# One-layer hybrid decoder with a mixture of experts on one core: gathers one block ahead in the first pair, a register load moved behind pair 10, squares summed on VectorE

## The chip, the cores and the metric

The kernel runs on one core of one Trainium2 chip. The metric is the device time of one execution in microseconds (us), the median of several runs. The engines are named as in the profile: PE is TensorE's matmul, PEld its weight load, DVE is VectorE, ACT is ScalarE, POOL is GpSimd, SP is SyncE, whose queue issues the loads of the weights here. A name with a q behind it (PEq, SPq) is an engine's sequencer: branches, register loads, issues of transfers.

## The reference

One layer is computed on 256 tokens of 1024 numbers:

```python
mod = silu(c) @ W_ada + b_ada            # shift, scale and gate of both sub-layers
h   = rmsnorm(x) * (1 + scale1) + shift1
proj = h @ w_in                          # 9224 columns: attention, mLSTM, gates
merged = sigmoid(g_a) * (y_a @ w_a) + sigmoid(g_b) * (y_b @ w_b)
x  += gate1 * (merged @ w_out)
h   = rmsnorm(x) * (1 + scale2) + shift2
x  += gate2 * moe(h)                     # the best 4 of 32 experts, clamped SwiGLU, D_FF = 1024
out = rmsnorm(x)                         # final norm
```

All of it is float32. What the change touches is the second norm (the mean of the squares of x over its 1024 channels), and the mixture of experts behind it.

## The kernel before

**Layout.** The residual stream lies transposed in `xT`, as KT = 8 blocks of 128 channels (on the partitions) by T = 256 tokens. A block is called kt.

**The w_out stage.** `merged @ w_out` is made in four chunks c of two blocks each. For each block the loop adds the gated product to `xT` (L754, DVE), scales it for the norm (L756, DVE), squares it into `sq` (L758, ACT), and then gives PE three things: the router's logits (L761, two matmuls that add up in one bank over the eight blocks), the mean of the squares (L765, two matmuls of `sq` with a column of 1/1024, also added up over the eight blocks), and the transposes of the scaled block (L768). The norm, the choice of the best four experts and the rank of each token in its expert follow on DVE, POOL, ACT and PE.

**The experts.** They are taken in 16 pairs. An expert has 64 slots in a pair's main pass; `G` (L819) is a matrix of ones and zeros that says which token sits in which slot. A pair p has these steps on PE:

- `biases`: four matmuls `s<-b1s,sel` that start the four banks of the first product with the bias;
- a gather per block (`pm<-G,mghi`), by which the slots' tokens are picked out of the normed rows `xn` (a tile called mghi), and which ACT copies to `XG[p]` with the shift added (L878);
- `first_product`: for each block and each half hf, four matmuls `s<-w,xg` with 128x512 of weights;
- SwiGLU on DVE and ACT, transposes, then `second_product`, 32 matmuls `t<-w,whi`;
- the scatter of the result to `xT` (`add_out`, matmuls `pm<-S,whi` and additions on DVE, L867), which is done during the first product of the next pair.

From pair 1 on, the gather of a pair is done in the pair ahead of it. In pair 0 there is no pair ahead: for each block the loop issues one gather and then the first product of this block. `pe()` keeps the matmuls of this part in the order in which the program gives them; all are recorded under L850.

**The weights.** A pair needs 12 loads of 2 MB: 8 for the first product (L949), 4 for the second (L954). They go by SP's queue, in order, into a ring of wide slots; a load waits on SP until the matmuls that read its slot before are done. Pair 0 is loaded apart, in halves (L943), since some of the ring's slots come free only during it. SP's instructions run in order, so a load that waits holds up all behind it.

**Further rounds.** An expert with over 64 tokens needs more slots. The largest count becomes `nit`, a number of rounds (L1066, DVE); `values_load` (L1067) reads it into a register on each of the five engines. Behind pair 10 (`REST_AT`) stands the branch that uses it (L1114): with zero rounds, as with these inputs, its body is skipped. Where nothing orders an instruction otherwise, a scheduler places it, for each engine apart.

Of the kernel before, what the change touches and what calls it, by code (L numbers as in the profile page):

```python
# [2 lines left out]

# [1 line left out]

# [5 lines left out]
F32 = mybir.dt.float32  # L14
# [5 lines left out]
OP = mybir.AluOpType  # L20
# [3 lines left out]
T = 256  # L24
D = 1024
KT = 8
# [37 lines left out]
def body(tc, a, out):  # L64
    nc = tc.nc
    mm = nc.tensor.matmul
    act = nc.scalar.activation
    tt = nc.vector.tensor_tensor
    ts = nc.vector.tensor_scalar
    stt = nc.vector.scalar_tensor_tensor  # L70
# [16 lines left out]
    def shaped(x, shape):  # L87

        n = int(np.prod(shape[1:]))
        names = "abc"[:len(shape) - 1]  # L90
        x = x[:, 0:n]
        if len(names) == 1:
            return x
        return x.rearrange(f"p ({' '.join(names)}) -> p {' '.join(names)}", **dict(zip(names[1:], shape[2:])))

    def next_wide():

        spare_half.clear()
        p = slots.pop(0)
        slots.append(p)  # L100
        return p.tile([128, 4 * D], F32, name="w")

    def next_slot(shape):

        if not spare_half:
            w = next_wide()
            spare_half.append(w[:, 2 * D:])
            return shaped(w, shape)
        return shaped(spare_half.pop(), shape)
# [8 lines left out]
    xT = const.tile([128, KT, T], F32, name="xT")  # L118
# [9 lines left out]
    mean = const.tile([128, 128], F32, name="mean")  # L128
# [10 lines left out]
    SH1, SC1, G1, SH2, SC2, G2 = range(6)  # L139
# [34 lines left out]
    for n in range(2):  # L174
        pz = ps_z.tile([128, 2, 512], F32, name="pz")[:, 0]
        b = slice(512 * n, 512 * n + 512)
# [22 lines left out]
    def mod_of(m, kt):  # L199
        return modT[:, 8 * m + kt:8 * m + kt + 1]  # L200
# [58 lines left out]
    def take():  # L259
        if not ready:  # L260
            fetch()
        return ready.pop(0)
# [255 lines left out]
    for c in range(4):  # L518
# [21 lines left out]
        for n in range(2):  # L540
# [22 lines left out]
            for x in (hi, lo):  # L563
                last = x is lo
# [78 lines left out]
    def read_out(hd, S):  # L643
        num = ps_z.tile([128, 2, 512], F32, name="pz")
        hn = mx.tile([128, 2, 256], F32, name="cs")
        st = mx.tile([128, 5, 2], F32, name="st")
        for t in range(2):
            for s in range(t + 1):
                mm(num[:, t, 0:257], S[:, 128 * t + 128 * s:128 * t + 128 * s + 128], ve[:, s, 0:257],
                   start=s == 0, stop=s == t)  # L650
        den = num[:, :, 256]
        stt(st[:, 0], den, -1.0, em[:, :, hd], OP.mult, OP.max)
        tt(st[:, 0], st[:, 0], den, OP.max)
        nc.vector.reciprocal(st[:, 1], st[:, 0])
        for t in range(2):
            sq = mx.tile([128, T], F32, name="sq")
            act(sq, num[:, t, 0:256], AF.Square, scale=st[:, 1, t:t + 1], accum_out=st[:, 2, t:t + 1])
        ts(st[:, 3], st[:, 2], 1.0 / 256, EPS, op0=OP.mult, op1=OP.add)
        nc.gpsimd.tensor_tensor(st[:, 3], st[:, 3], half, OP.pow)
        tt(st[:, 4], st[:, 1], st[:, 3], OP.mult)  # L660
        for t in range(2):
            ts(hn[:, t, :], num[:, t, 0:256], st[:, 4, t:t + 1], None, op0=OP.mult)
        return hn
# [15 lines left out]
    last = None  # L679
    for hd in range(4):  # L680
# [6 lines left out]
        last = hd, read_out(hd, S), so  # L687
# [41 lines left out]
    wk, c_wk = pool("wk", reuse_waits="tile")  # L729
# [3 lines left out]
    pl = ps_m.tile([128, 512], F32, name="pm")  # L733
# [9 lines left out]
    for c in range(4):  # L743
        w = take()
        if c < 3:
            ps = proj_T(w, (mghi, mglo))
            fetch()
            po = [ps[:, 0, :], ps[:, 1, :]]
        else:
            po = proj_apart(w, (mghi, mglo))  # L750
        px = ps1.tile([128, 512], F32, name=f"s{c}").rearrange("p (t n) -> p t n", t=2)
        for n in range(2):
            kt = 2 * c + n
            stt(xT[:, kt, :], po[n], mod_of(G1, kt), xT[:, kt, :], OP.mult, OP.add)  # L754
            x = xa[c // 2][:, kt % 4, :]
            ts(x, xT[:, kt, :], A2[:, kt:kt + 1], None, op0=OP.mult)  # L756
            sq = wk.tile([128, T], F32, name="GS"[n])
            act(sq, xT[:, kt, :], AF.Square)  # L758
            for t in range(2):
                b = slice(128 * t, 128 * t + 128)  # L760
                mm(pl[:, 32 * t:32 * t + 32], x[:, b], rw[:, kt, :], start=False, stop=kt == KT - 1,  # L761
                   skip_group_check=True)
            for t in range(2):
                b = slice(128 * t, 128 * t + 128)
                mm(pl[:, 96 + t:97 + t], sq[:, b], mean[:, 0:1], start=False, stop=kt == KT - 1,  # L765
                   skip_group_check=True)
            for t in range(2):
                nc.tensor.transpose(px[:, t, 128 * n:128 * n + 128], x[:, 128 * t:128 * t + 128], ident)  # L768
        if c < 3:
            act(xtok[c // 2][:, c % 2], px, AF.Copy)  # L770
        later((0,0,0,0,)[c])
# [53 lines left out]
    XG, SS, ROWS = {}, {}, {}  # L825
    G0, last = slots_of(0)
# [21 lines left out]
    def pe(*args, **kw):  # L848

        return tc.keep_in_program_order(mm(*args, **kw))  # L850
# [8 lines left out]
    def add_out(lhsT_of, rhs, groups=range(4)):  # L859

        for g in groups:
            p = ps_m.tile([128, 2, T], F32, name="pm")
            for j in range(2):
                pe(p[:, j, :], lhsT_of(2 * g + j), rhs, start=True, stop=True)
            for j in range(2):
                kt = 2 * g + j
                stt(xT[:, kt, :], p[:, j, :], mod_of(G2, kt), xT[:, kt, :], OP.mult, OP.add)  # L867

    def gather(kts, G, xg):

        width = G.shape[-1]
        p = ps_m.tile([128, 512], F32, name="pm")
        for j, kt in enumerate(kts):
            c = slice(128 * kt, 128 * kt + 128)
            for t in range(2):
                pe(p[:, width * j:width * j + width], xn[:, t, c], G[:, t], start=t == 0, stop=t == 1)
        for j, kt in enumerate(kts):
            act(xg[kt] if isinstance(xg, list) else xg[:, kt, :], p[:, width * j:width * j + width], AF.Identity, bias=mod_of(SH2, kt))  # L878
# [132 lines left out]
    def pair(p):  # L1011
        a1 = biases(p)
        aT = halves([128, 4, 128]) if p else None
        if p == 0:
            for kt in range(KT):
                gather((kt,), G0, XG[0])
                for hf in range(2):
                    first_product(p, a1, hf, kt)
            scatter_map(p)
            aT = halves([128, 4, 128])  # L1020
            ms = [hidden(a1, hf) for hf in range(2)]
            G, _ = slots_of(p + 1)
            gather(range(4), G, XG[p + 1])
            turn(ms[0], 0, aT)
            gather(range(4, 8), G, XG[p + 1])
            m = ms[1]
        else:
            for kt in range(KT):
                first_product(p, a1, 0, kt)
                if p - 1 in ROWS and 1 <= kt <= 4:  # L1030
                    scatter(p - 1, (kt - 1,))
            m = hidden(a1, 0)
            for kt in range(KT):
                first_product(p, a1, 1, kt)
                if kt == 1:
                    scatter_map(p)
                if kt == 3:
                    turn(m, 0, aT)
            m = hidden(a1, 1)
            G, _ = slots_of(p + 1)  # L1040
            for q in range(2):
                gather(range(4 * q, 4 * q + 4), G, XG[p + 1])
        a2 = [ps2.tile([128, 512], F32, name=f"t{n}") for n in range(2)]
        for kt in range(KT):
            if kt == 4:
                turn(m, 1, aT)
            second_product(p, a2, aT, kt)
        ROWS[p] = out_rows(a2)
# [12 lines left out]
    nit = moe.tile([1, 1], I32, name="nit")  # L1061
# [2 lines left out]
    ts(cnt[:, 1:2], cnt[:, 0:1], float(CAP + 128), None, op0=OP.is_gt)  # L1064
    stt(cnt[:, 1:2], cnt[:, 0:1], float(CAP), cnt[:, 1:2], OP.is_gt, OP.add)
    nc.vector.tensor_copy(nit, cnt[0:1, 1:2])  # L1066
    rounds = nc.values_load(nit, min_val=0, max_val=2)  # L1067

    rest5 = rest.rearrange("p r t (q e) -> p r t q e", e=2)
    gate4 = gate.rearrange("p t (q e) -> p t q e", e=2)  # L1070
# [38 lines left out]
        rows = out_rows(a2)  # L1109
        add_out(lambda kt: block(rows, kt), S)  # L1110

    def rest_of_slots():
        ws = [next_slot([128, 2 * D]) for _ in range(5)]
        with tc.If(rounds > 0):  # L1114
            with tc.For_i(0, rounds, 1) as r:
                with tc.For_i(0, NE // 2, 1) as q:
                    for e in range(2):
                        more(r, q, e, ws)

    for p in range(NE // 2 - 1):  # L1120
        pair(p)
        if p == 1:
            b2 = xgp.tile([128, D], F32, name="xh")[0:32]
            nc.sync.dma_start(b2, a["b2"])
        if p == 3:
            add_b2(b2)
        if p == REST_AT:
            scatter(p)
            del ROWS[p]
            rest_of_slots()  # L1130


    p = NE // 2 - 1
# [33 lines left out]
    sqs, done = [], []  # L1167
# [51 lines left out]
    for g in (3, 0, 1, 2):  # L1219
        b = xo[:, 2 * g:2 * g + 2, :]  # L1220
# [71 lines left out]
```

## Time and profile before

| | us |
|---|---|
| median of 3 runs (lowest to highest) | 1301.83 (1301.69 to 1302.64) |
| the profiled execution, its own time | 1301.86 |
| span of its trace | 1300.2 |
| PE busy | 1217.3 (94% of the span) |
| DVE busy | 466.2 (36%) |
| ACT busy | 337.4 (26%) |
| moved by DMA | 483.41 MB, mean 372 GB/s |

Times in the trace count from the start of the span; 1.66 us of the execution lie outside it. PE is the busiest engine over the whole span, but the stages differ: the first 370 us make the mixers, the rest the experts, whose weights are most of the bytes.

### The profile page before, as it was taken

Reading aid. Unit: us, or ns where it says so; the run is one execution under the profiler, and the core shown is the slowest. Engines: PE = TensorE matmul, PEld = TensorE weight load, DVE = VectorE, ACT = ScalarE, POOL = GpSimd, SP = SyncE. Lnnn points to the kernel's source line nnn. Section 1 sums busy time; section 2 is a strip of 40 time slices with the busy share of each in tenths; the row PEclk is TensorE's granted clock in tenths of the full one; section 3 lists DMA queues with packets and bytes.
Section 4 is the critical chain, followed back from the end, with each engine's and each line's share of the span. In section 5 each row is a group of like instructions: output and inputs, shape, how many; then the busy total and the mean of one; then the engine's idle time right before and its main releaser. Section 6 shows DMA issues by size and latency. Waiting matters only on the chain.

```text
span 1300.2 us, 16506 instructions
## 1 busy us (share of the span) xinstructions
PE 1217.3 (94%) x6859; PEld 670.4 (52%) x6874; DVE 466.2 (36%) x911; ACT 337.4 (26%) x626; POOL 32.5 (3%) x63
## 2 busy tenths in 40 slices
PE   7999999999979999999999998998988998989987
PEld 6988999999933334333334433333333333333333
DVE  7898999865522213123121211212121212212013
ACT  4578877555412010110101101010101101010102
POOL 2000000000000000000000000000000000000002
PEclk8999999999999999999999999999999999999999
DMA  9966555675778999999999999999999999999995
GB/s 357 368 223 255 214 225 231 249 315 214 295 285 359 402 423 426 427 428 426 427 428 426 426 428 427 428 425 426 427 427 425 428 428 427 427 426 427 428 422 212
DMA packets 44989, 483.41 MB, mean 372 GB/s; under 512 B 5318, under 2 KB 6742, under 8 KB 10860
## 3 DMA queue, kind: packets, MB, share of 16 engines
q1 hardware_dynamic: 43740, 480.53, 89.1%
q0 software_dynamic: 624, 1.23, 0.4%
q8 instruction: 56, 0.92, 0.3%
q10 hardware_dynamic: 544, 0.52, 0.1%
q14 instruction: 25, 0.20, 0.0%
HBM read 481.21 MB, written 1.05 MB: 371 GB/s over the span
## 4 chain that ended last, share of the span: by engine, by line
PE 58%; DMA 35%; DVE 3%; ACT 3%; issue 1%; POOL 0%; SPq 0%; DVEq 0%; POOLq 0%; ACTq 0%
DMA w<-in_w 32%; PE s L850 19%; PE t L850 9%; PE pm L850 6%; PE pj L274 4%; PE pj L276 4%; PE pj L275 4%; DMA w<-in_w_last 2%; PE pz L402 2%; PE pm L853 1%; PE pj L402 1%; DMA w<-in_w_first 1%; PE pj L303 1%; PE pj L304 1%; PE pj L305 1%
## 5 line engine op out<-in xcount | busy, mean ns | idle before, releaser
L850 PE MATMUL s<-w,xg 128*64 128x512 f32 x2032 | 464.2, 599 | 35.2 <-DMA w<-in_w 32.0
L850 PEld LDWEIGHTS s<-w,xg 128*64 128x64 f32 x2032 | 135.0, 137 | 303.1 <-issue 240.4
L850 PE MATMUL t<-w,whi 128*64 128x512 f32 x948 | 212.4, 596 | 11.0 <-ACT whi L901 9.6
L867 DVE SCALAR_TENSOR_TENSOR xT<-pm,modT,xT 128x256 f32<-128x256 f32 x128 | 56.0, 480 | 386.6 <-PE pm L850 386.6
L850 PEld LDWEIGHTS t<-w,whi 128*64 128x64 f32 x948 | 65.1, 137 | 136.6 <-issue 114.0
L885 ACT ACTIVATE wlo<-wlo 128x512 f32<-128x512 f32 x32 | 20.1, 629 | 416.6 <-DVE wlo L883 416.6
L240 DVE TENSOR_TENSOR wlo<-w,whi 128x512 fp32r<-128x512 f32 x164 | 109.5, 687 | 40.1 <-ACT whi L238 39.6
L238 ACT ACTIVATE whi<-w 128x512 fp32r<-128x512 f32 x162 | 100.6, 630 | 76.2 <-PE pj L275 63.0
L883 DVE TENSOR_SCALAR wlo<-s 128x512 f32<-128x512 f32 x32 | 22.1, 691 | 243.2 <-PE s L850 228.0
L274 PE MATMUL pj<-hhi,whi 128*128 128x256 f32 x368 | 105.2, 286 | 2.4 <-ACT sgate L712 1.1
L276 PE MATMUL pj<-hhi,wlo 128*128 128x256 f32 x368 | 104.9, 285 | 0.3 <-DVE wlo L240 0.3
L275 PE MATMUL pj<-hlo,whi 128*128 128x256 f32 x368 | 104.4, 284 | 0.0
L274 PEld LDWEIGHTS pj<-hhi,whi 128*128 128x128 f32 x368 | 70.4, 191 | 3.7 <-ACT whi L238 1.4
L276 PEld LDWEIGHTS pj<-hhi,wlo 128*128 128x128 f32 x368 | 70.4, 191 | 1.1 <-DVE wlo L240 0.7
L275 PEld LDWEIGHTS pj<-hlo,whi 128*128 128x128 f32 x368 | 70.4, 191 | 0.2
L850 PEld LDWEIGHTS pm<-G,mghi 128*128 128x128 f32 x512 | 59.5, 193 | 17.9 <-issue 17.3
L850 PE MATMUL pm<-S,whi 128*128 128x256 f32 x240 | 67.3, 404 | 0.2 <-DVE xT L867 0.2
L850 PEld LDWEIGHTS pm<-S,whi 128*128 128x128 f32 x240 | 40.8, 189 | 50.1 <-issue 39.5
L850 PE MATMUL pm<-G,mghi 128*128 128x128 f32 x512 | 63.8, 280 | 0.2 <-ACT xg L878 0.2
L901 ACT ACTIVATE whi<-pm 128x512 f32<-128x512 f32 x32 | 19.1, 597 | 163.2 <-PE pm L853 163.2
L187 DVE CUSTOM_DVE_ANT_0 w<-w,silr,col 128x1024 f32<-128x1024 f32 x48 | 60.4, 1279 | 0.6 <-ACT silr L700 0.5
L878 ACT ACTIVATE xg<-pm,modT 128x128 f32<-128x128 f32 x128 | 37.1, 368 | 68.9 <-PE pm L850 68.9
(372 smaller groups left out, 1293.1 us busy)
## 6 DMA issues: line engine op xcount, KB each, us to landing
w<-in_w SPq DMA_DIRECT2D x176, 2048.0 KB, 35.9
w<-in_w_in SPq DMA_DIRECT2D x29, 1024.0 KB, 7.8
w<-in_ada SPq DMA_DIRECT2D x22, 1024.0 KB, 7.0
w<-in_w SPq DMA_DIRECT2D x20, 1024.0 KB, 8.8
w<-in_w_first SPq DMA_DIRECT2D x7, 896.0 KB, 14.9
w<-in_w_last SPq DMA_DIRECT2D x6, 1024.0 KB, 27.1
w<-in_w_a SPq DMA_DIRECT2D x4, 1024.0 KB, 10.5
w<-in_w_b SPq DMA_DIRECT2D x4, 1024.0 KB, 12.9
```

The source lines that it names most:

```text
L187: nc.vector.tensor_tensor_reduce(out=w[:, j + n, :], in0=w[:, j + n, :], in1=SILU[-1], scale=1.0, scalar=col[:, C_AB + i:C_AB + i + 1], op ...
L238: act(hi, x, AF.Copy)
L240: nc.vector.tensor_tensor(lo, x, f32(hi), OP.subtract)
L274: mm(ps[:, n, :], whi[:, j, s], mhi[:, kt, :], start=kt + n == 0, stop=False, skip_group_check=True)
L275: mm(ps[:, n, :], whi[:, j, s], mlo[:, kt, :], start=False, stop=False, skip_group_check=True)
L276: mm(ps[:, n, :], wlo[:, j, s], mhi[:, kt, :], start=False, stop=last, skip_group_check=True)
L402: order.append(mm(first[c][:, n, :], l, r, start=kt + n + i == 0, stop=kt == KT - 1 and i == 2, skip_group_check=True).ins)
L850: return tc.keep_in_program_order(mm(*args, **kw))
L867: stt(xT[:, kt, :], p[:, j, :], mod_of(G2, kt), xT[:, kt, :], OP.mult, OP.add)
L878: act(xg[kt] if isinstance(xg, list) else xg[:, kt, :], p[:, width * j:width * j + width], AF.Identity, bias=mod_of(SH2, kt))
L883: ts(g, glu, LIMIT, None, op0=OP.min)
L885: act(s, g, AF.Sigmoid, scale=ALPHA)
```

## The change

It has three parts. The squares of blocks 0 to 6 are added up on DVE, and only their sum and the square of block 7 go through the matmuls of the mean. In pair 0 the gather of a block stands one block ahead of its first product. The register load stands in `rest_of_slots`, and by `issue_after` behind the last matmul and the last addition of pair 10's scatter; `issue_after` orders instructions that share an engine and adds no wait between engines.

```diff
             x = xa[c // 2][:, kt % 4, :]
             ts(x, xT[:, kt, :], A2[:, kt:kt + 1], None, op0=OP.mult)
-            sq = wk.tile([128, T], F32, name="GS"[n])
+            sq = wk.tile([128, T], F32, name="GS"[n] if kt else "sq")
             act(sq, xT[:, kt, :], AF.Square)
+            if kt == 0:
+                sqs = sq
+            elif kt < KT - 1:
+                tt(sqs, sqs, sq, OP.add)
             for t in range(2):
                 b = slice(128 * t, 128 * t + 128)
                 mm(pl[:, 32 * t:32 * t + 32], x[:, b], rw[:, kt, :], start=False, stop=kt == KT - 1,
                    skip_group_check=True)
-            for t in range(2):
+            for t in range(2 if kt > KT - 3 else 0):
                 b = slice(128 * t, 128 * t + 128)
-                mm(pl[:, 96 + t:97 + t], sq[:, b], mean[:, 0:1], start=False, stop=kt == KT - 1,
+                mm(pl[:, 96 + t:97 + t], (sqs if kt < KT - 1 else sq)[:, b], mean[:, 0:1], start=False, stop=kt == KT - 1,
                    skip_group_check=True)
...
-                pe(p[:, j, :], lhsT_of(2 * g + j), rhs, start=True, stop=True)
+                last = pe(p[:, j, :], lhsT_of(2 * g + j), rhs, start=True, stop=True)
...
-                stt(xT[:, kt, :], p[:, j, :], mod_of(G2, kt), xT[:, kt, :], OP.mult, OP.add)
+                added = stt(xT[:, kt, :], p[:, j, :], mod_of(G2, kt), xT[:, kt, :], OP.mult, OP.add)
+        LASTS[:] = [last.ins, added.ins]
...
         if p == 0:
+            gather((0,), G0, XG[0])
             for kt in range(KT):
-                gather((kt,), G0, XG[0])
+                if kt < KT - 1:
+                    gather((kt + 1,), G0, XG[0])
                 for hf in range(2):
                     first_product(p, a1, hf, kt)
...
-    rounds = nc.values_load(nit, min_val=0, max_val=2)
...
-    def rest_of_slots():
+    def rest_of_slots(behind):
         ws = [next_slot([128, 2 * D]) for _ in range(5)]
+        with contextlib.ExitStack() as stack:
+            for i in behind:
+                stack.enter_context(tc.issue_after(i))
+            rounds = nc.values_load(nit, min_val=0, max_val=2)
         with tc.If(rounds > 0):
...
-            rest_of_slots()
+            rest_of_slots(LASTS)
```

The order of PE's instructions in chunk 0 of the w_out stage, before: `rw` is the router's matrix, `mean` the column of 1/1024, `G` and `S` the two tiles of squares, `cst` the identity of the transposes.

```order
L761 MATMUL pm<-rw,xg 128x32 x2
L765 MATMUL pm<-mean,G 128x1 x2
L768 MATMUL s_4018<-cst,xg 128x128 x2
L761 MATMUL pm<-rw,xg 128x32 x2
L765 MATMUL pm<-mean,S 128x1 x2
L768 MATMUL s_4018<-cst,xg 128x128 x2
L276 MATMUL pj<-mghi,wlo 128x256
```

The same place in the changed kernel, where the lines of the file are 6 further on (2 for the products `pj`):

```order
L767 MATMUL pm<-rw,xg 128x32 x2
L774 MATMUL s_4018<-cst,xg 128x128 x2
L767 MATMUL pm<-rw,xg 128x32 x2
L774 MATMUL s_4018<-cst,xg 128x128 x2
L278 MATMUL pj<-mghi,wlo 128x256
```

The two rows of the mean are gone; the router's matmuls and the transposes stand as before.

The order of PE's instructions at the start of pair 0, before: the bias matmuls, then the gather of block 0 and its first product.

```order
L850 LDWEIGHTS sel
L1067 TENSOR_LOAD nit
L850 MATMUL s_4423<-b1s,sel 128x512
L850 LDWEIGHTS sel
L850 MATMUL s_4425<-b1s,sel 128x512
...
L850 MATMUL pm<-G,mghi 128x128 x2
L850 MATMUL s_4423<-w,xg 64x512 x2
L850 MATMUL s_4425<-w,xg 64x512 x2
L850 MATMUL s_4424<-w,xg 64x512 x2
L850 MATMUL s_4426<-w,xg 64x512 x2
L850 MATMUL pm<-G,mghi 128x128 x2
```

And in the changed kernel:

```order
L856 LDWEIGHTS sel
L856 MATMUL s_4403<-b1s,sel 128x512
L856 LDWEIGHTS sel
L856 MATMUL s_4405<-b1s,sel 128x512
...
L856 MATMUL pm<-G,mghi 128x128 x4
L856 MATMUL s_4403<-w,xg 64x512 x2
L856 MATMUL s_4405<-w,xg 64x512 x2
L856 MATMUL s_4404<-w,xg 64x512 x2
L856 MATMUL s_4406<-w,xg 64x512 x2
L856 MATMUL pm<-G,mghi 128x128 x2
```

The register load no longer stands ahead of the first bias matmul, and two gathers (blocks 0 and 1) stand ahead of the first product in place of one.

The order of SP's instructions around the branch behind pair 10 in the changed kernel (before, the register load stood among pair 0's loads, in the middle of those of L943):

```order
L963 DMA w<-in_w 128x4096 x4
L958 DMA w<-in_w 128x4096 x8
L963 DMA w<-in_w 128x4096 x4
L1127 TENSOR_LOAD nit
L1127 ISA x2
L958 DMA w<-in_w 128x4096 x2
L1128 COMPARE_AND_BRANCH
```

On SP the register load now stands behind all 12 loads of pair 10 and ahead of the first two of pair 11, which are issued ahead of the branch as before.

## Rows read from the trace of the kernel before

**Rows 1.** The chain that ended last: shares of the span by line.

```profile
DMA w<-in_w 32%; PE s L850 19%; PE t L850 9%; PE pm L850 6%; PE pj L274 4%; PE pj L276 4%; PE pj L275 4%; DMA w<-in_w_last 2%; PE pz L402 2%; PE pm L853 1%; PE pj L402 1%; DMA w<-in_w_first 1%; PE pj L303 1%; PE pj L304 1%; PE pj L305 1%
```

**Rows 2.** Busy time by stretch, columns in the first line.

```profile
core 0: us, PE busy (x) PEld busy (x) DVE busy (x) ACT busy (x) POOL busy (x), PEclk, DMA share, GB/s
331.00:358.00 27.00, 27.00 (x236) 26.76 (x237) 12.38 (x26) 11.44 (x22) 0.18 (x1) 1.00 0.84 346
367.00:374.00 7.00, 5.32 (x21) 2.56 (x23) 0.90 (x6) 0.37 (x1) 0.29 (x1) 0.76 0.06 26
368.00:371.00 3.00, 2.50 (x7) 1.49 (x7) 0.00 (x0) 0.24 (x1) 0.29 (x1) 0.50 0.03 11
374.00:412.00 38.00, 33.85 (x168) 13.65 (x164) 5.02 (x12) 6.49 (x16) 0.00 (x0) 1.00 1.00 411
412.00:416.00 4.00, 4.00 (x26) 2.50 (x28) 1.84 (x5) 1.44 (x5) 0.00 (x0) 1.00 0.08 33
416.00:430.00 14.00, 13.15 (x63) 4.38 (x60) 0.00 (x0) 1.79 (x3) 0.00 (x0) 1.00 0.94 352
...
750.00:1278.00 528.00, 481.20 (x2246) 181.25 (x2254) 92.56 (x190) 56.25 (x130) 2.05 (x7) 1.00 1.01 427
```

**Rows 3.** PE in order of time, one block in the w_out stage: start, us, operation.

```profile
337.04 0.58 PE L765 MATMUL pm<-mean,G 128*128 128x1 f32 x4
337.49 0.41 PE L768 MATMUL s<-cst,xg 128*128 128x128 f32 x2
```

**Rows 4.** DVE in order of time, an operation on two 128x256 tiles.

```profile
330.38 0.42 DVE L735 TENSOR_TENSOR S<-rw,modT 128x256 f32<-128x256 f32 x1
```

**Rows 5.** The tile nit: durations in ns, first and last start in us.

```profile
L1066 DVE CAST nit<-cnt x1: 135/135/135, 367.3 to 367.3; 1x1 int32<-1x1 f32 x1
L1067 PEldq TENSOR_LOAD <-nit x1: 485/485/485, 367.5 to 367.5; - x1
L1067 SPq TENSOR_LOAD <-nit x1: 477/477/477, 375.5 to 375.5; - x1
```

**Rows 6.** PE in order of time, the start of pair 0; in brackets the idle time ahead.

```profile
363.62 0.38 PE L169 MATMUL t<-onesb 128*128 128x512 bf16 x1
368.00 1.01 PE L850 MATMUL s<-b1s,sel 128*128 128x512 bf16 x2 [4.01 <-DVE rw L926]
...
369.67 1.06 PE L850 MATMUL pm<-G,mghi 128*128 128x128 f32 x4
371.18 3.68 PE L850 MATMUL s<-w,xg 128*64 128x512 f32 x16 [0.46 <-ACT xg L878]
```

**Rows 7.** DVE in order of time, the slots of pair 0.

```profile
364.08 0.49 DVE L819 TENSOR_TENSOR G<-rank,cst 128x128 f32<-128x128 f32 x2
```

**Rows 8.** PE in order of time, three later places at full clock.

```profile
403.31 0.71 PE L850 MATMUL pm<-G,mghi 128*128 128x128 f32 x4
404.48 1.94 PE L850 MATMUL s<-whi,xg 128*64 128x512 f32 x8 [0.46 <-ACT xg L878]
...
411.87 2.05 PE L850 MATMUL pm<-G,mghi 128*128 128x128 f32 x16 [0.21 <-ACT xg L878]
...
456.90 7.09 PE L850 MATMUL s<-w,xg 128*64 128x512 f32 x32
```

**Rows 9.** SP in order of time, the first load that waited for pair 0.

```profile
373.19 0.33 SPq L943 DMA_DIRECT2D w<-in_w  x1
```

**Rows 10.** The tile w, 405 to 435 us: issues on SP of pair 1's loads.

```profile
L949 SPq DMA_DIRECT2D w<-in_w x3: 328/328/328, 415.8 to 425.9; - x3
```

**Rows 11.** The line of the branch behind pair 10.

```profile
L1114 PEldq COMPARE_BRANCH  x1: 6060/6060/6060, 996.3 to 996.3; - x1
```

**Rows 12.** PE in order of time, around this branch.

```profile
989.71 3.65 PE L850 MATMUL t<-w,whi 128*64 128x512 f32 x16 [0.21 <-DMA w<-in_w]
...
995.48 1.97 PE L850 MATMUL pm<-S,whi 128*128 128x256 f32 x8 [0.20 <-DVE xT L867]
1002.64 1.80 PE L850 MATMUL s<-b1s,sel 128*128 128x512 bf16 x4 [5.19 <-PEq L1114]
```

More of the change, by code (lines that the diff above doesn't have):

```diff
@@ L7 @@
+import contextlib
 import numpy as np
@@ L863, in add_out @@
             for j in range(2):
-                pe(p[:, j, :], lhsT_of(2 * g + j), rhs, start=True, stop=True)
+                last = pe(p[:, j, :], lhsT_of(2 * g + j), rhs, start=True, stop=True)
             for j in range(2):
                 kt = 2 * g + j
-                stt(xT[:, kt, :], p[:, j, :], mod_of(G2, kt), xT[:, kt, :], OP.mult, OP.add)
+                added = stt(xT[:, kt, :], p[:, j, :], mod_of(G2, kt), xT[:, kt, :], OP.mult, OP.add)
+        LASTS[:] = [last.ins, added.ins]
+    LASTS = []
     def gather(kts, G, xg):
```

## The prediction

> **What bounds the kernel now.** I read the chain that ended last first: a third of it is loads of weights, the rest PE, the experts' lines and the projections [rows 1]. So there are two regimes, and the windows by stage say where they meet [rows 2]. In the w_out stage (331 to 358 us) PE is busy 27.00 of 27.00 us, and the DMA line is not full (0.84). From 374 us on, when pair 0 begins to give slots back, the line is full (1.00) for 38 us, nearly empty from 412 to 416 (0.08), at 0.94 to 430, and at 750 to 1278 us at 1.01 and 427 GB/s, while PE is busy 481.20 of 528.00 us. The reader is to see in this that the end is set by one line of transfers in SP's order: it starts when the first product of pair 0 frees its first slot, has one hole, and then runs to the last load. Behind it lie 22 us of last products and the final norm, which the change doesn't touch. A microsecond is won at the end if the line starts earlier or if its hole is closed; PE work saved after 430 us would be worth nothing.
>
> All sums go against the profiled execution, 1301.86 us (span 1300.2, 1.66 around it), 0.03 over the median. About 0.2%, 2.6 us, is what a measurement of this kernel can tell from no change.
>
> **Squares on VectorE.** Six of eight pairs of mean matmuls go, 24 records of PE. One block's four start at 337.04 and the next operation at 337.49 [rows 3], 0.45 us; six are 2.7. The modelled duration of 0.58 would make 3.5, and the stage's mean of 27.00/236 = 0.114 per record [rows 2] 2.75; I take 2.7. In exchange DVE adds six times two 128x256 tiles, at 0.42 each [rows 4], 2.5 us, while it is busy 12.38 of these 27 us: hidden by PE's projections of the next chunk. Without that cover, in the last chunk, where the sum for block 6 stands ahead of PE, one or two of them are bare, 0.42 or 0.85; so the bounds are 1.8 and 3.5. The line could follow: with 0.84 of 27 us it needs 22.7.
>
> **The register load at pair 0.** `nit` is written by a cast on DVE at 367.32 us, PE's sequencer then loads it for 485 ns from 367.5 [rows 5], and the first bias matmul starts at 368.00, after 4.01 idle [rows 6]. All of the biases' other needs are older: the last matmul ahead of them started at 363.62, and `G` is there at 364.08 + 0.49 = 364.57 [rows 7]. The granted clock in 368 to 371 is 0.50, the lower level of 1.2 GHz, behind this idle time; afterwards it is 1.00 [rows 2]. So the four biases took 369.67 − 368.00 = 1.67, at full clock about 0.84. After the change: biases from about 363.84, gather of block 0 at 364.70, 0.71 at full clock [rows 8], ACT's copy 0.46 [rows 6], first product at 365.9 in place of 371.18: **5.3**. The second gather, now ahead of it too, lies under the 0.46 of ACT; if it takes 0.71, it costs 0.25. Bounds 5.0 and 5.3, and 0 if the load isn't what PE waits for (below).
>
> **Gathers one block ahead.** From the first product of block 0 (371.18) to that of block 7 (404.48) are seven steps of 4.757. In each, gather and wait take 404.48 − 403.31 = 1.17 [rows 8], so the 16 matmuls 3.59; 32 later ones took 7.09, which agrees. After the change ACT's 0.46 is behind matmuls; what is left is the gather itself, between 0.71 (the row) and what one adds in a run of four, (2.05 − 0.71)/3 = 0.45 [rows 8]. I take the middle, 0.58, since a gather between other matmuls has its weight loads partly hidden. Six steps of 3.59 + 0.58 and a last one without a gather, 3.59, are 28.6 in place of 33.3: 4.7, bounds 4.0 and 5.5. So PE reaches the second product of pair 0 5.3 + 4.7 = 10 us earlier, besides the 2.7.
>
> **What of it reaches the end.** Counted from the end of the w_out stage: the first load that waits for pair 0 is issued at 373.19 [rows 9], and the line is full from 374. Both come 5.3 earlier, and the 38 us of loads end at about 406.7. Pair 1's first three loads are issued at 415.8 to 425.9, as the second product frees slots [rows 10]; 10 earlier is 405.8 and 415.9, while a load of 2 MB at 427 GB/s takes 4.9, so two loads last from 406.7 to 416.5. The hole closes: of its 4 × 0.92 = 3.7 and the 14 × 0.06 = 0.8 behind it, I leave 0.3. The line's end moves by 2.7 + 5.3 + 4.5 − 0.3 = **12.2**. PE's own gain, 12.7, is a little more, so the line is still what ends last: 1301.9 − 12.2 = **1289.7**. With the bounds of the terms (line: 1.8 + 5.0 + 3.5 to 3.5 + 5.3 + 4.5) it is 1288.6 to 1291.6.
>
> **The register load at pair 10.** On PE it adds 0.48 ahead of the branch, which takes 6.06 [rows 11] and holds the biases of pair 11 until 1002.64 [rows 12]. The cover is PE's slack: over 750 to 1278 us it idles 47 us for the line [rows 2], and the loads of pair 11 come from SP meanwhile. Without that cover it costs 0.48. On SP it stands ahead of pair 11's first two loads, another 0.48 + some 0.2 of checks; behind it wait all later loads. `nit` is hundreds of microseconds old then, and the line is at 1.01 there [rows 2], fed from loads issued before, so it costs nothing. At pair 0, SP's own load of 477 ns at 375.5 [rows 5] goes.
>
> **The rivals.**
>
> *A: the biases wait for something else.* The profile names a DVE instruction of L926 as what ended the 4.01 us [rows 6], not the register load. If they wait for that, the 5.3 stays and the line starts 2.7 earlier only, with its hole closed: 2.7 + 4.5 = 7.2, 1294.7 us. Against it: in the order of PE the load stands right ahead of the bias matmul, and it ends at 367.5 + 0.49 = 367.99, the matmul starts at 368.00. Chance 0.08.
>
> *B: the hole only moves.* From 374 to 412 the line moved 411 GB/s, not 427 [rows 2], and if second-product releases come later than I move them, it is dry as long as before: 2.7 + 5.3 = 8.0, 1293.9 us. Against it: the first of these loads was issued at 415.8 [rows 10], and the stretch of 0.08 ends at 416, so the hole does end on PE's release. Chance 0.10.
>
> *C: nothing reaches the end.* If the line were full all the way from pair 0's first loads, PE's gains would go into waiting: 1301.9. For it is that over 750 us of the span the line is full. Against it are the stretches at 0.06 and 0.08 [rows 2]. Chance 0.06. The Trainium skill speaks for this rival (Perfetto Trace Analysis, section Identifying the Most-Contended Engine): the engine to be optimized first is the one with the highest occupancy, and for DMA one goes by HBM utilization; none of the three parts moves a byte less, so by it the sum would be 0 and the time 1301.9. The same page's section Optimization Strategy sends one to the gaps within that engine's regime and to what would end them sooner; by that, and the two stretches are such gaps here, the sum is the 12.2.
>
> *D: slower: the register load stops SP at pair 10.* SP stands at it with all loads of pair 11 behind. If it is held until the engines are through the branch (PE's biases at 1002.64), the line runs dry after pair 10's last load, which PE waited for at 989.71 [rows 12]: 1002.64 + 0.7 for the load and its checks + 0.8 from issue to flow (as from 373.19 to 374) − 989.7 = 14.4 of dry line, against 12.2 gained: 1304.1. Held until the biases of pair 11 have run as well, 1002.64 + 1.80, it is 16.2 and 1305.9; only until the scatter's last matmuls are done, 995.48 + 1.97 = 997.45, it is 9.3 and 1299.0. It loses from 1000.4 on, and over 0.2% from 1003.0. For it: the load is ordered behind the scatter on PE and DVE. Against: that order is within each engine, the order of SP has it behind loads alone, and what the load needs is the cast. Chances: 0.03 for 1305.9, 0.01 for 1304.1, 0.02 for 1299.0.
>
> **How the numbers follow.** Forecast 0.70; its own range is 1288.6 to 1291.6, which I take down to 1288.0, since PE's terms at their upper bounds (3.5 + 5.3 + 5.5 = 14.3) allow 1287.6. With B the range must reach 1293.9, which makes 0.80, and I end it at 1294.2; A, C and D are left out. Faster: forecast, A, B and the mildest D, 0.90; same: C and the middle D, 0.07; slower: 0.03.
>
> **What would show it.** PE: six blocks of the mean fewer, the w_out stage 2.7 shorter. No idle time of microseconds ahead of the first bias, clock 1.00 in the biases; first product 2.3 behind the last warm-up matmul (363.62 to 365.9); its steps 4.2 and the 0.46 gone. DMA share near 1 through what was 412 to 416. Last loads' landing 12 earlier, the tail as long as before. At pair 10 PE waits 0.5 more at the branch, with the line at 1.01. The prediction is wrong if the 4 us stay (A), if a stretch of low DMA share follows pair 0 (B), or if one appears at pair 11's loads (D).

## The result and the profile after

The changed kernel takes 1288.96 us (median of 4 runs, 1288.60 to 1289.64) against 1301.76 for the kernel before (4 runs): a ratio of 0.9898, 95% interval 0.9886 to 0.9910, 12.8 us less. Measured again with the last experiments it was 1289.31 against 1301.84, ratio 0.9902 (0.9886 to 0.9917). Forecast were 1289.7 and 1288.0 to 1294.2. The profiled execution took 1288.98, its span is 1287.3.

First the windows by stage of the changed kernel, with the columns of [rows 2]:

```profile
core 0: us, PE busy (x) PEld busy (x) DVE busy (x) ACT busy (x) POOL busy (x), PEclk, DMA share, GB/s
361.00:364.00 3.00, 2.95 (x22) 1.90 (x23) 2.93 (x15) 0.73 (x2) 0.29 (x1) 1.00 0.99 364
364.00:368.00 4.00, 4.00 (x20) 1.44 (x18) 1.51 (x9) 0.36 (x1) 0.00 (x0) 1.00 0.69 232
368.00:402.00 34.00, 33.05 (x174) 14.48 (x172) 6.80 (x16) 6.50 (x17) 0.00 (x0) 1.00 1.01 417
402.00:412.00 10.00, 9.31 (x46) 3.15 (x44) 0.07 (x1) 1.31 (x4) 0.00 (x0) 1.00 0.99 398
412.00:416.00 4.00, 4.00 (x22) 1.41 (x20) 0.00 (x0) 0.00 (x0) 0.00 (x0) 1.00 0.94 381
416.00:430.00 14.00, 14.00 (x62) 4.88 (x58) 2.63 (x6) 1.19 (x2) 0.29 (x1) 1.00 1.00 417
738.00:1266.00 528.00, 484.50 (x2268) 182.72 (x2268) 92.57 (x190) 57.00 (x130) 2.05 (x7) 0.99 1.01 426
```

The granted clock is 1.00 in 361 to 430 us; before it was 0.50 in 368 to 371 [rows 2]. From 368 us the line of transfers is full and stays so: no stretch answers to the 0.08 of before, the lowest share of these windows is 0.94. PE in order of time shows what replaced the start of pair 0. Its first row is the last of the warm-up matmuls (L171), products of a tile of ones whose result is not used:

```profile
361.17 0.38 PE L171 MATMUL t<-onesb 128*128 128x512 bf16 x1
361.38 1.02 PE L856 MATMUL s<-b1s,sel 128*128 128x512 bf16 x4
362.24 1.05 PE L856 MATMUL pm<-G,mghi 128*128 128x128 f32 x8
363.31 3.65 PE L856 MATMUL s<-w,xg 128*64 128x512 f32 x16
366.89 0.71 PE L856 MATMUL pm<-G,mghi 128*128 128x128 f32 x4
367.54 3.65 PE L856 MATMUL s<-w,xg 128*64 128x512 f32 x16
...
392.15 1.89 PE L856 MATMUL s<-whi,xg 128*64 128x512 f32 x8
...
399.48 0.71 PE L856 MATMUL pm<-G,mghi 128*128 128x128 f32 x4 [0.21 <-ACT xg L887]
```

The last row is cut off by the end of this view, at 400 us. No row behind the first has idle time ahead of it until 398.64, where PE waits 0.73 for DVE's SwiGLU. The biases start 0.21 behind the last warm-up matmul; before it was 4.38 [rows 6]. The first product starts 2.14 behind it, before 7.56. From there to the first product of block 7 are 28.84 us, before 33.30 [rows 6, 8]. SP's first loads that waited for pair 0, and the last wait for weights:

```profile
365.29 0.33 SPq L952 DMA_DIRECT2D w<-in_w  x1
365.66 0.43 SPq L952 DMA_DIRECT2D mglo<-in_w  x1
```

```profile
1265.15 1.95 PE L1187 MATMUL t<-w,whi 128*64 128x256 f32 x16 [0.42 <-DMA w<-in_w_last]
```

The first waiting load is issued 7.90 us earlier than before [rows 9]. The matmuls of the last row stood here before:

```profile
1278.03 1.95 PE L1173 MATMUL t<-w,whi 128*64 128x256 f32 x16 [0.43 <-DMA w<-in_w_last]
```

They start 12.88 earlier; what follows takes the same 22.2 us in both spans. Behind pair 10 the branch and the biases after it read:

```profile
L1128 PEldq COMPARE_BRANCH  x1: 6432/6432/6432, 984.1 to 984.1; - x1
```

```profile
990.83 1.44 PE L856 MATMUL s<-b1s,sel 128*128 128x512 bf16 x3 [6.15 <-PEq L1128]
```

PE waits 6.15 there, before 5.19 [rows 12]: of the 0.96 more, 0.49 is the register load and 0.37 a branch that happened to take 6.43 in place of 6.06. It left no gap in the line, as the window around it says (columns of [rows 2]):

```profile
980.00:992.00 12.00, 5.65 (x23) 3.29 (x20) 4.82 (x14) 0.97 (x2) 0.00 (x0) 0.90 1.01 425
```

Behind this wait PE's granted clock is 0.50 in 990 to 996 us, before it was so in 1003 to 1006; the line is full in both stretches (1.00 and 1.02).

### The profile page after: what moved, and what is told of

It is laid out like the page before. It is cut to its first block, busy times and chain, and to the rows that moved or that the text cites. A ratio compares the mean times of both kernels' runs of the same rounds, so it can differ in the third digit from the quotient of the medians.

```text
span 1287.3 us, 16479 instructions
## 1 busy us (share of the span) xinstructions
PE 1217.2 (95%) x6850; PEld 666.9 (52%) x6850; DVE 468.4 (36%) x917; ACT 337.4 (26%) x626; POOL 32.4 (3%) x63
## 3 DMA queue, kind: packets, MB, share of 16 engines
HBM read 481.21 MB, written 1.05 MB: 375 GB/s over the span
## 5 line engine op out<-in xcount | busy, mean ns | idle before, releaser
L856 PE MATMUL t<-w,whi 128*64 128x512 f32 x948 | 212.4, 596 | 12.2 <-ACT whi L910 9.6
## 6 DMA issues: line engine op xcount, KB each, us to landing
w<-in_w_first SPq DMA_DIRECT2D x7, 896.0 KB, 14.7
w<-in_w_a SPq DMA_DIRECT2D x4, 1024.0 KB, 10.5
```

## The experiments

All times are medians beside the kernel before on the same chip, which gave 1301.81, 1301.48 and 1301.84 in the three sets; in brackets stand the ratio to it and its 95% interval.

**Each part alone.** `sum_alone`, `load_alone` and `gather_alone` are the kernel before with one part of the diff each. The core of the three edits, cut short, with comments that name the kernel:

```diff
+                tt(sqs, sqs, sq, OP.add)                            # sum_alone, with its matmuls
...
-    rounds = nc.values_load(nit, min_val=0, max_val=2)              # load_alone
+            rounds = nc.values_load(nit, min_val=0, max_val=2)      # in rest_of_slots
...
+            gather((0,), G0, XG[0])                                 # gather_alone
-                gather((kt,), G0, XG[0])
+                    gather((kt + 1,), G0, XG[0])
```

> Only the squares are summed on VectorE; gathers and register load as before. If the transfer line follows PE (its start waits for pair 0's first product), everything behind the w_out stage comes 2.5 us earlier: 1299.3 us, with the first warm-up matmul before pair 0 at about 361.2 instead of 363.62 and the low DMA share still there behind the first product. If the line were full anyway, 1301.8.

Measured: 1299.30 (ratio 0.9979, 0.9970 to 0.9988). The line does follow PE: the load `mglo`, the second on SP that waits for pair 0, is issued at 371.56 us, before at 373.56.

> Only the register load is moved. If it is what the biases of pair 0 wait for, they start at about 363.8, the first product 5.3 us earlier, and the line's start with it, while its hole between the first and the second product stays as wide as before: 1296.5 us. If the biases wait for the DVE instructions of the scatter map, 4 us of idle stay and the time is 1301.8.

Measured: 1296.39 (0.9960, 0.9946 to 0.9973), 5.4 less. The biases start 0.21 behind the last warm-up matmul, so rival A, by which they wait for the instructions of the scatter map, is out, though the profile names one of these as what ended the wait [rows 6]. The hole stays, as its windows show:

```profile
404.00:408.00 4.00, 3.05 (x26) 2.65 (x25) 4.00 (x10) 3.70 (x9) 0.00 (x0) 1.00 1.01 430
408.00:412.00 4.00, 4.00 (x26) 2.17 (x27) 1.25 (x4) 1.14 (x4) 0.00 (x0) 1.00 0.05 20
412.00:416.00 4.00, 4.00 (x22) 1.18 (x18) 0.00 (x0) 0.00 (x0) 0.00 (x0) 1.00 0.95 328
```

The columns are those of [rows 2]. The hole has moved from 412 to 408 with the rest of the line and is as wide as before.

> Only the gathers of pair 0 stand one block ahead. The line's first waiting load is issued as before (373.2, or some tenths later for the second gather), the seven steps of the first product lose 4.5 us, and the hole of 4 us closes: 4.2 to 4.5 us, 1297.4 us. If the hole only moves, or the loads behind it are late anyway, 1301.8.

Measured: 1299.17 (0.9978, 0.9969 to 0.9987), only 2.6 less: a miss. The hole did close, but the windows of this kernel, and PE in order of time, show what the expectation left out:

```profile
371.00:374.00 3.00, 3.00 (x12) 1.54 (x13) 0.00 (x0) 0.73 (x2) 0.00 (x0) 0.50 0.02 5
...
408.00:412.00 4.00, 3.31 (x24) 2.62 (x26) 3.30 (x9) 2.35 (x9) 0.00 (x0) 1.00 1.00 426
412.00:416.00 4.00, 4.00 (x20) 1.29 (x18) 0.00 (x0) 0.55 (x3) 0.00 (x0) 1.00 0.98 352
```

```profile
364.22 0.38 PE L169 MATMUL t<-onesb 128*128 128x512 bf16 x1
368.61 1.86 PE L850 MATMUL s<-b1s,sel 128*128 128x512 bf16 x4 [4.01 <-DVE rw L926]
370.26 1.91 PE L850 MATMUL pm<-G,mghi 128*128 128x128 f32 x8
372.11 4.69 PE L850 MATMUL s<-w,xg 128*64 128x512 f32 x16
```

With the register load where it was, PE still sits idle for 4.01 us, and the clock is 0.50 until 374. The two gathers take 1.85 there, to the next row's start, and 1.07 in the changed kernel; the first product takes 4.69 and not 3.65. The gathers, and 3.02 us of this product, lie ahead of the issue of the first waiting load (375.13).

**Each part left out.** `no_sum`, `no_gather` and `no_load` are the changed kernel with one of those three edits undone, as the same lines of the diff with + and - exchanged.

> The change without the squares on VectorE (register load and gathers as changed). If the three parts add up, it is 2.5 us slower than the changed kernel: 1291.4 us. If the line has slack that covers this part, 1289.0.

Measured: 1292.90 (0.9929, 0.9916 to 0.9943).

> The change without the gathers ahead. The line starts as early as in the changed kernel (about 365.3 us) but its hole behind the first product is back, some 4 us of it: 4.5 to 5 us slower than the changed kernel, 1293.7 us. If the line's start alone decides, 1289.0.

Measured: 1293.17 (0.9933, 0.9919 to 0.9946).

> The change without the moved register load. If the parts add up, 5.3 us slower than the changed kernel, 1294.3 us, and the same as the kernel in which PE alone loads the register early. If moving it on SP is worth something of its own, this one is slower than that one.

Measured: 1295.34 (0.9947, 0.9934 to 0.9961). Against the 1288.96 and 1289.31 of the whole change, which ran in other sets, the squares are worth some 3.5 to 4, the gathers about 4, the register load about 6: each more than alone (2.5, 2.6, 5.4). But a single ratio has an interval of ±1.2 to 1.8 us, so the medians don't show for which part this is real. For the squares the traces don't show it: the last warm-up matmul starts at 363.95 in `no_sum`, at 361.17 and 361.37 in the two traces of the changed kernel, 2.6 to 2.8 later, and the table finds no difference behind it. Two quantities of each trace tell the parts apart better than the medians. I take from the start of the last warm-up matmul (361.17 in the changed kernel) the issue of the load `mglo` on SP (365.66) and the start of the second half of pair 1's gathers on PE (399.48):

| kernel | to the load | to these gathers |
|---|---|---|
| before | 9.94 | 48.25 |
| sum_alone | 10.34 | 48.65 |
| load_alone | 4.49 | 42.79 |
| gather_alone | 11.28 | 45.10 |
| no_sum | 4.49 | 38.31 |
| no_gather | 4.49 | 42.82 |
| no_load | 11.12 | 44.95 |
| changed | 4.49 | 38.31 |

The register load alone gives 5.46 at the gathers, the gathers alone 3.15, both 9.94, which is 1.33 more than the sum. And the line's start is the same with and without the gathers ahead when the register load is out of the way (4.49), but 1.34 later with them when it is not. (The 0.40 that `sum_alone` has over the kernel before is clock too: its first product took 4.08, before 3.68 [rows 6].)

**Where PE's register load sits.** `pe_early` is the changed kernel with

```diff
     nc.vector.tensor_copy(nit, cnt[0:1, 1:2])
+    nc.values_load(nit, engines=[mybir.EngineType.PE], min_val=0, max_val=2)
```

> The changed kernel with one more register load, on PE alone and ahead of pair 0's biases (its value is not used); SP's and all others stay behind pair 10. If PE's register load is the whole of that part, the 4 us of idle and the clock of 0.50 return, and it loses about 5.3 us against the changed kernel: 1294.3 us. If it was SP's register load among pair 0's loads, it stays at 1289.0.

Measured: 1296.91 (0.9960, 0.9947 to 0.9974), on the chip of the first set. The 4 us of idle (4.39) are back, the clock is 0.50 in 364 to 370 us, and its two quantities of the table are 10.90 and 44.73, within 0.22 of those of `no_load`. So PE's register load is the whole of that part in the trace. The medians of the two kernels, 1296.91 and 1295.34, come from two sets whose intervals overlap and tell nothing of SP's share.

**The clock apart from the wait.** `warm_before` and `warm_gather` are the kernel before and `gather_alone` with

```diff
     warm(4, idle)
+    for _ in range(20):
+        tc.keep_in_program_order(mm(idle, onesb, onesb[:, None, :].to_broadcast([128, 4, 128]), start=True, stop=True))
```

> The kernel before with 20 more warm-up matmuls on PE between the ranks and the register load of pair 0, some 4.3 us of work while PE would wait. If the low clock behind the wait is a price of its own, the biases and the first gather run at 1.00, about 1.2 to 1.3 us less: 1300.5 us, the wait itself staying. If the clock makes nothing at the end, 1301.8.

Measured: 1300.13 (0.9989, 0.9980 to 0.9998).

> The gathers alone, with the same 20 warm-up matmuls. If the parts alone do not add up because the second gather and the first products then lie in the stretch of low clock, this gives back what is missing: from the last warm-up matmul of before to the second product 44.5 us in place of 47.1, and 1296.6 us. If the missing part has another cause, it stays at 1299.2.

Measured: 1296.44 (0.9957, 0.9944 to 0.9971). PE in order of time in `warm_gather`, and a window with the columns of [rows 2]:

```profile
364.12 4.48 PE L804 MATMUL t<-onesb 128*128 128x512 bf16 x20
368.43 1.03 PE L852 MATMUL s<-b1s,sel 128*128 128x512 bf16 x4
369.30 1.05 PE L852 MATMUL pm<-G,mghi 128*128 128x128 f32 x8
370.36 3.65 PE L852 MATMUL s<-w,xg 128*64 128x512 f32 x16
```

```profile
368.00:371.00 3.00, 2.99 (x19) 1.88 (x19) 0.19 (x1) 0.74 (x2) 0.29 (x1) 1.00 0.06 19
```

Work without use in the place of the wait keeps the clock at 1.00, and the gathers then take 1.06 and the product 3.65, with the register load still there. The quantities of the table are 8.81 and 47.12 in `warm_before`, 8.81 and 42.64 in `warm_gather`: the clock costs 1.13 without the gathers ahead and 2.46 with them. The biases start 0.15 later than without the warm-up matmuls (368.45 − 363.92 = 4.53 in `warm_before`, 4.38 before), so both are net of that. The difference, 1.33, is what the parts alone lacked at these gathers: with the clock held, the gathers ahead are worth 4.48, as they are when the register load is moved. The 1.33 is no fixed price: between `sum_alone` and `no_load` the gathers are worth 48.65 − 44.95 = 3.70, so there 0.78 is lacking. And the medians lack 2.0 to 2.3; whether more than the clock is in that is not shown, since it is near what single intervals allow.

**The slower rival made true.** `hold_first` is the changed kernel with the lines below, in which `SPL` holds SP's register load. The copy stands on DVE behind pair 10's scatter, and each load of pair 11's first product behind that register load.

```diff
-        nc.sync.dma_start(w, w1[p, hf, k2].rearrange("p j e b n -> p (j e b n)"))
+        d = nc.sync.dma_start(w, w1[p, hf, k2].rearrange("p j e b n -> p (j e b n)"))
+        if p == REST_AT + 1:
+            for i in SPL:
+                tc.add_manual_dep(d.ins, i.ins.name, mybir.DependencyInfo(
+                    mybir.DependencyClass.NoSync, mybir.DependencyReason.DATA))
...
-            rounds = nc.values_load(nit, min_val=0, max_val=2)
+            nc.vector.tensor_copy(nit2, nit)
+            loads, (rounds,) = nc.values_load_multi_w_load_instructions(nit2, min_val=0, max_val=2)
```

> The changed kernel, but the register load behind pair 10 reads a copy of nit that VectorE writes behind the last addition of pair 10's scatter, and all loads of pair 11 are ordered behind SP's register load. This makes the slower rival come true in its milder form: the line runs dry from the landing of pair 10's last load (about 976.9 us) until the register load is done and the next load flows (984.7 + 1.5): about 9.3 us lost, 1298.3 us, with a stretch of low DMA share there. If later slack of PE or the ring takes it up, less than that; if nothing waits for these loads, 1289.0.

Measured: 1303.35 (1.0015, 1.0006 to 1.0025), 14.0 to 14.7 over the changed kernel, which ran in other sets (14.0 by its second median as it stands, 14.7 by the differences from the kernel before). Windows of this kernel around the scatter of pair 10:

```profile
969.00:972.00 3.00, 3.00 (x16) 0.92 (x13) 0.00 (x0) 0.00 (x0) 0.00 (x0) 1.00 0.94 399
972.00:975.00 3.00, 2.31 (x14) 0.93 (x14) 0.00 (x0) 0.60 (x1) 0.00 (x0) 1.00 0.55 235
975.00:987.00 12.00, 9.34 (x42) 4.26 (x38) 3.52 (x9) 1.19 (x2) 0.00 (x0) 1.00 0.02 10
987.00:990.00 3.00, 0.00 (x0) 0.02 (x1) 0.16 (x1) 0.00 (x0) 0.00 (x0) 0.52 0.68 164
```

```profile
L1132 DVE COPY nit<-nit x1: 130/130/130, 985.6 to 985.6; 1x1 int32<-1x1 int32 x1
L1133 SPq TENSOR_LOAD <-nit x1: 476/476/476, 985.8 to 985.8; - x1
```

The line was empty for 3 × 0.06 + 3 × 0.45 + 12 × 0.98 + 3 × 0.32 = 14.2 us, about what is lost at the end: a microsecond of dry line is a microsecond of time. I had counted from PE's wait for the last load, which ends at 977.03 in this trace; the line thins out from 972 and is empty from 976. And the copy starts at 985.6, behind DVE's last addition, not at the end of PE's scatter (984.77), and the next load is issued at 987.17, where I had counted with a flow from 986.2.

`hold_later` is the same without the order put on pair 11's loads, so that SP issues two of pair 11's loads ahead of the register load.

> As the kernel that holds SP's register load behind pair 10's scatter, but with pair 11's first two loads left ahead of it on SP. They feed the line for 9.8 us more, from about 974.2 to 984.0; the register load, the branch and the next issue are through at about 987.4 to 988: 3.4 to 4 us of dry line, 1292.7 us. If the hold costs something that is not the dry line, it stays at 1303.

Measured: 1294.00 (0.9936, 0.9921 to 0.9951), 4.7 over the changed kernel. Its windows:

```profile
981.00:984.00 3.00, 2.80 (x13) 2.01 (x12) 1.61 (x4) 0.67 (x2) 0.00 (x0) 1.00 0.65 279
984.00:987.00 3.00, 1.38 (x7) 0.85 (x5) 1.91 (x6) 0.00 (x0) 0.00 (x0) 1.00 0.18 76
987.00:990.00 3.00, 0.00 (x0) 0.00 (x0) 0.00 (x0) 0.00 (x0) 0.00 (x0) 0.78 0.64 126
```

3 × (0.35 + 0.82 + 0.36) = 4.6 us of empty line, and 4.7 lost.

**The change again.**

> The changed kernel once more, for a comparison with the kernels that leave one part out at more rounds. 1289.0 us, 12.8 less than before, if the first measurement holds; the parts alone (2.5 + 5.4 + 2.6 = 10.5) do not add up to that, so 1291.3 if they should and the first was lucky.

Measured: 1289.31, as told at the top. The parts alone make 10.5, the whole 12.5 and 12.8 in its two sets.

## Why the prediction was right

The forecast was 12.2, the measurement 12.8 and 12.5, by the mechanism that it named: the line's start and its hole.

**Squares on VectorE**, 2.7: from the router's first matmuls of the w_out stage (336.57 before, 336.90 after) to the last warm-up matmul are 27.05 and 24.27 us, 2.78 less. Alone it gave 2.5. The two rows, before and after:

```profile
336.57 0.63 PE L761 MATMUL pm<-rw,xg 128*128 128x32 f32 x4
336.90 0.63 PE L767 MATMUL pm<-rw,xg 128*128 128x32 f32 x4
```

**The register load at pair 0**, 5.3: the first product came from 7.56 to 2.14 behind the last warm-up matmul, 5.42, a little over the bounds of 5.0 to 5.3: gather and ACT take 1.07 where I had 0.71 + 0.46, and the second gather costs nothing (2.14 in `load_alone` too). Both halves of the term are seen apart: `warm_before` takes a net 1.13 of clock from it and leaves the wait.

**Gathers ahead**, 4.7: measured 4.46 between the first products of blocks 0 and 7. A gather between products costs 367.54 − 366.89 = 0.65, not the 0.58 that I took as the middle.

**What reaches the end**, 12.2: the line's start moved by 7.90, forecast 8.0 with the squares. The rest, 12.88 − 7.90 = 4.98, is the hole; I had left 0.3 of its 4.5 open. The repeat's trace has its first waiting load at 365.49 and the last wait at 1266.19, 0.8 longer than the first trace's line; by it the same remainder is 4.14. So the forecast's 4.2 for the hole lies within what two executions give, and they don't tell it closer.

**The rivals.** A and C fell with `load_alone` and `sum_alone`. Two gaps of the line gave back 7.90 and 4.98 us, while the bytes read from memory stayed at 481.21 MB. The Trainium skill (Perfetto Trace Analysis, section Optimization Strategy) says to look for the gaps on the engine of the regime and for what would end them sooner; the trace agrees by these two numbers. B, the hole that only moves, is what `load_alone` shows when the gathers stay behind. D was right as a mechanism and its price was too low: I had 9.3 for a hold until the scatter, `hold_first` measured 14.0 to 14.7, enough to make the whole change slower than before. It did not happen, because the changed kernel's register load reads `nit` itself: SP went through it at 938.6 us, some 40 us before the scatter:

```profile
L1127 SPq TENSOR_LOAD <-nit x1: 480/480/480, 938.6 to 938.6; - x1
```

**What the working lacked** did not show in the forecast: the three terms were summed without a word on which of them needs another. The sum holds for all three together, but the gathers' 4.7 needs the register load out of the way: with the register load in its old place the gathers ahead are worth 2.6, since they then run at the low clock and delay the line's start by 1.34.

## What to carry to other kernels

Where a full line of transfers sets the end, count what moves its start and what closes its gaps; here some 12.7 us of PE's time, saved ahead of and in one stretch (2.78 + 9.94), came back nearly whole at the end. Behind 430 us they would have met a line at 1.01 [rows 2], where I expect nothing of them; no run tried it. A small load of a register holds all that its engine has behind it; give it a place where its source is old, and look on every queue at what stands behind. Parts of a change that meet in one stretch are not to be summed from runs of each alone: an idle engine that comes back at half clock makes the next part's work dearer.

## What was not expected of the hardware

The stretch of low clock (0.50, 1.2 GHz) behind the 4 us wait was not of one length. In the kernel before it is 0.50 from 368 to 371 us and 0.86 in the next microsecond; in `gather_alone` it is 0.50 from 368 to 374 and 0.88 in the next. That PE is busy without a pause from 368.61 on in `gather_alone`, while the kernel before has 0.46 of idle time between gather and product, doesn't account for it: `sum_alone` has this idle time too, and its clock is 0.50 from 363 us, when PE still waited, to 369, and 0.66 in the next. What sets the length was not tried.

The taken branch behind pair 10 was shorter where the line was empty. In the twelve traces whose line is full there it took 5.97 to 7.19 us on PE (50 to 72 ns on the other engines); in `hold_first`, where the line was empty when it began, the page of its line reads

```profile
L1135 PEldq COMPARE_BRANCH  x1: 3332/3332/3332, 986.4 to 986.4; - x1
```

and 3.63 in `hold_later`. The Trainium skill (Runtime: NRT & Kernel Launch, section Instruction fetch mechanics) says that a taken branch out of the window that has been read ahead waits for a fetch by DMA. The trace agrees: in each of the fourteen traces a packet of 16 KB of instructions is moved while PE's branch lasts. In 996.3 to 1002.4 us of the kernel before the queue's packets, MB and share of the 16 engines are

```profile
q8 instruction: 1, 0.02, 1.1%
```

In the ten full-line traces with one such packet it starts 3.50 to 3.95 us behind the branch's start and takes 1.02 to 1.11; `gather_alone` and `pe_early`, with the longest branches (7.19 and 6.96), have two. In `hold_first` and `hold_later` it starts after 1.01 and 1.31 us and takes 1.00 and 1.02. From its end to the branch's end are 1.30 to 1.56 us in all fourteen. So the shorter branch is a shorter wait for the packet. That the weights ahead of it in the line are what it waits for fits the two kernels against the twelve; it isn't shown apart from that.
